# Expert gates of a two-block transformer kernel: one-hot rows made per token with scalar operands

## The chip, the cores and the metric

The kernel runs on one core of a Trainium2 chip. The metric is the device time in microseconds. Three runs of the kernel before gave 3348.83 us (median), between 3345.13 and 3349.56. All rows below come from one profiled execution, whose span is 3351.7 us.

## The reference, cut to what matters

256 tokens of 1024 channels go through a first block (attention and feed-forward layers) and a second block of two layers, each a mixer and then an expert layer (`peer_ffn`). The change touches the expert layer alone:

```python
def peer_ffn(h, w_q, sub_keys, u_tab, v_tab):
    q = (h @ w_q).reshape(B, S, PEER_HEADS, 2, PEER_DQ // 2)
    scores = jnp.einsum('bshpd,hpkd->bshpk', q, sub_keys)
    s1, i1 = lax.top_k(scores[..., 0, :], PEER_TOPK)
    s2, i2 = lax.top_k(scores[..., 1, :], PEER_TOPK)
    ...
    ids = jnp.take_along_axis(cand_id, top_pos, axis=-1)
    gate = jax.nn.softmax(top_s, axis=-1)
    ...
        u = u_tab[idx]
        act = jax.nn.gelu(jnp.einsum('thkd,td->thk', u, hx))
        return jnp.einsum('thk,thkd->td', g * act, v_tab[idx])
```

There are 128 x 128 experts, and a token picks 8 heads x 16 of them. An expert's number has two halves, i1 and i2, each below 128.

## The kernel before, in words

The kernel does not gather experts. For each of 128 tiles of 128 experts it computes the activations of all tokens (`u_tile`, L1661), keeps them in `M` (128 experts of a tile on partitions, 128 tiles, 256 tokens), multiplies them by a dense gate (zero for experts that a token did not pick), and multiplies the result by the second table (`accumulate`, L1358). A tile of u costs 24 products on PE, 8 input channels by 3 passes, since every float32 weight is split into two parts, `hi` and `lo`. `hi` is made by ACT (L262), `lo` by POOL or DVE (L263): in the stretch with gates the pattern `lo_pat` is "PVPVP", three of five on POOL and two on DVE. The weights come over SP's queue in 512 KB pieces; there are three buffers each for `raw`, `hi` and `lo`.

The dense gates are made four tokens at a time (`gates(g)`, 64 groups in a layer). The 128 picks of a token lie on partitions. `CT` holds the two halves of the expert number, `W3` the weight as three bfloat16 parts. Comparing a half with 0 to 127 (`iota`) gives, for each pick, a one-hot row of 128; `oh[:, 0]` has the rows of the second half, `first` those of the first half, and `oh[:, 1:4]` is `first` times the three weight parts. PE multiplies the one-hot matrix of the second half (stationary) with the three weighted ones (moving) into a quarter of a PSUM bank for each token: 12 products for a group. DVE then multiplies the u tiles that are already in `M` by these gates (L1656), and ACT writes the gates into the rest of `M` (L1658), where later u tiles are multiplied in (L1666, L1669, L1670).

Before the change the tile `oh` is laid out [partition, kind, one-hot column, token]: the token is innermost, so a token's row has its elements four apart (8 bytes). Three wide DVE instructions make a group: two compares of 512 elements (L1645) and one multiplication of 1536 (L1646).

A program that schedules by its own costs sets the order in which the instructions of an engine stand; every engine then works through its own in that order. The budgets in the loop (0.85 groups of gates for a u tile) fix the mix of gates and tiles: 27 tiles pass while the picks are found, then about 75 tiles go with the 64 groups, then 26 come alone.

Of the kernel before, what the change touches and what calls it, by code (L numbers as in the profile page):

```python
# [12 lines left out]
BF16 = mybir.dt.bfloat16  # L13
U32 = mybir.dt.uint32
AF = mybir.ActivationFunctionType
ALU = mybir.AluOpType
# [156 lines left out]
class Kernel:  # L173
# [33 lines left out]
    def input_tiles(self):  # L207
        # beside the tokens two columns, for the products with vectors
        self.XHc, self.XLc = (self.cp.tile([128, KT, T + 2], F32R, name=n, tag=n) for n in ("XH", "XL"))
        self.XH, self.XL = self.XHc[:, :, :T], self.XLc[:, :, :T]  # L210
# [29 lines left out]
    def ps(self, tag="mm", n=None):  # L240
        """One of the eight banks: four in turn for each of two uses, or a certain one."""
        if n is None:
            n = self.bank[tag] % 4
            self.bank[tag] += 1
        return self.pp.tile([128, 512], F32, name="ps_" + tag, tag=f"{tag}{n}", bufs=1)

    def lo_engine(self):
        if self.calm:
            # the first weights after a norm: not in the way of its VectorE work
            self.calm -= 1  # L250
            return self.nc.gpsimd
        e = self.lo_pat[self.lo_n % len(self.lo_pat)]
        self.lo_n += 1
        return self.nc.vector if e == "V" else self.nc.gpsimd
# [24 lines left out]
    @contextmanager  # L279
    def stream(self, raw, hi):  # L280
        """More room for the weights on their way while this lasts."""
        with self.tc.tile_pool(name="xraw", bufs=raw) as r, self.tc.tile_pool(name="xhi", bufs=hi) as h:
            self.seq = {"raw": [self.rawp] * 3 + [r] * raw, "hi": [self.hip] * 3 + [h] * hi}
            self.seq_n = {"raw": 0, "hi": 0}
            yield
        self.seq = {"raw": [self.rawp], "hi": [self.hip]}
# [20 lines left out]
    def linear(self, out, wsrc, kt, xin, chunk=8):  # L307
        mm = self.nc.tensor.matmul
        k0 = 0
        # which operand is the last to be there  # L310
        passes = ((0, 0), (1, 0), (0, 1)) if self.fresh else ((0, 0), (0, 1), (1, 0))
        while k0 < kt:
            n = min(chunk, kt - k0)
            w = self.first or self.wsplit(wsrc[:, k0:k0 + n, :], (n, 128))
            self.first = None
            order = [(i, k) for i in range(3) for k in range(n)]
            if self.fresh == "channels":
                # the inputs come, or go, one after the other
                order.sort(key=lambda o: o[1])
            elif self.fresh == "banks":  # L320
                order.sort(key=lambda o: (o[0] == 2, o[1] > 5))
            for at, (i, k) in enumerate(order):
                a, b = passes[i]
                mm(out, w[a][:, k], xin[b][:, k0 + k], start=k0 == 0 and at == 0,  # L324
                   stop=k0 + n == kt and at == 3 * n - 1)
            k0 += n
# [3 lines left out]
    def emit(main, side=(), rate=1.0):  # L330
        """Runs a generator, with the steps of others spread among its own."""
# [14 lines left out]
    def fill(self, n, after):  # L346
        """Some of the work that can be done at any time, but not before a tile is there."""
# [11 lines left out]
    def start(self, weights):  # L359
        """The input, and with it the first weights, in parts."""  # L360
# [23 lines left out]
    def sqrt_soon(self, pool, x):  # L384
        """Loads the square root's table once x is there, ahead of its use."""
# [16 lines left out]
    def layer_norm(self, pool, l, n, mid=(), then=None):  # L402
        """then: "raw" or "mod" if the products after it start before the norm is known (begin)."""
# [98 lines left out]
    def softmax(self, pool, parts, scale, guard, gate=None):  # L502
        """parts: (scores, bias, n) of rows side by side; all their probabilities in one tile."""
# [26 lines left out]
    def causal_pt(self, pool, score, bias, scale, gate=None):  # L530
        """Transposed probabilities: early queries, late queries on early keys, late on late."""
# [22 lines left out]
    def mem_keys(self, l):  # L554
        # one head's rows in each copy, zeros in the other's
# [11 lines left out]
    def natural(self, wsrc, x, store):  # L567
        """256 columns with the tokens on partitions."""
        nc = self.nc
        p = self.ps("ax")  # L570
        for c in range(2):
            hi, lo = self.wsplit(wsrc[:, 4 * c:4 * c + 4], (4, T))
            for k in range(4):
                kk = 4 * c + k
                for a in range(2):
# [3 lines left out]
                    # both halves of the bank form one group: its first product clears them  # L579
# [38 lines left out]
    # The attention of a mixer and its output projection: the sums of the projection stay in four banks, and each  # L618
    # 128 channels are added to them when their heads are done.
    def mix_start(self, l, mix):  # L620
        self.l, self.mix = l, mix
        self.ob = self.ps("ax", 3)
        # in the place of the mixer's input, which is not needed any more
# [7 lines left out]
    def mixed(self):  # L631
        """Half a bank for the outputs of two heads."""
# [4 lines left out]
    def project_out(self, i):  # L637
# [7 lines left out]
        for b in range(4):  # L645
            for w, x in ((hi, xh), (hi, xl), (lo, xh)):
                for k in (0, 1):
                    # the two halves of a bank form one group: its first product clears both
# [32 lines left out]
    def mla(self, l, mid=()):  # L681
        nc, tc, A = self.nc, self.tc, self.A
        with self.stream(2, 2), tc.tile_pool(name="mla", bufs=1) as pool:
# [9 lines left out]
            # per head: 64 rows without position, 32 rotated ones  # L693
            qt = pool.tile([128, 12, T], F32, name="qt")
            kt = pool.tile([128, 12, T], F32, name="kt")
            # what comes before the heads' parts, in their place
# [24 lines left out]
            # keys and values from the latent  # L721
# [21 lines left out]
            for c in range(3):  # L743
                hi, lo = self.wsplit(A["uq"][c], (4, 2, 128))
                # four heads: two tiles without position, their rotated rows, and those swapped
# [42 lines left out]
    def nsa_kv(self, pool, tp):  # L788
# [6 lines left out]
        # one group's rows in each copy, zeros in the other's  # L795
# [70 lines left out]
    def nsa(self, l):  # L866
        nc, tc, A = self.nc, self.tc, self.A
        kk, vv, kc, vc = self.nsakv
        with self.stream(2, 2), tc.tile_pool(name="nsa", bufs=1) as pool:
# [22 lines left out]
            # compressed branch  # L892
# [93 lines left out]
    # The products of a normalised input x r ac + sh start with x ac, before r is known: the products of the  # L986
    # first tiles are multiplied by r (a number per token) and get that of sh, a column beside the tokens, added.
# [30 lines left out]
    def begin(self, pool, srcs, hm=None, norm=True):  # L1018
        """The first products with a normalised input, before its norm is known; then that input in full."""
# [45 lines left out]
    def add_later(self, n=KT):  # L1065
        """What the input lacks yet of the normalised one, which only the residual needs."""
# [13 lines left out]
    def product(self, wsrc, pool, tmp=None):  # L1080
        """A tile of products with the normalised input, and a bias to be added to it."""
# [19 lines left out]
    def rms_sum(self, pool, gains=None):  # L1101
        """The sum of squares for a norm; the last one (with gains) at once for the whole of it."""
        nc, X = self.nc, self.X
        # a norm before this one may have left its shift to be added
# [30 lines left out]
    def hgrn(self, l):  # L1135
        nc, tc, A = self.nc, self.tc, self.A
        with self.stream(2, 1), tc.tile_pool(name="hg", bufs=1) as pool:
# [64 lines left out]
            def project(pr):  # L1202
# [7 lines left out]
                # Q[:, 0]: backward, Q[:, 1]: forward; K[:, 0]: forward, K[:, 1]: backward  # L1210
# [10 lines left out]
            def attend(pr):  # L1221
# [12 lines left out]
                for li, h in enumerate(LEVELS):  # L1234
# [11 lines left out]
                    # products of the decays over blocks of h, then the next level's operands  # L1246
# [75 lines left out]
    def prepare(self):  # L1322
        """What the second block needs from its parameters alone."""
        nc = self.nc
        # HGRN2's lower bounds: softmax over the one layer, then its exclusive sum
# [8 lines left out]
        # the convolution's taps  # L1334
# [5 lines left out]
        # softplus(-lam) = max(-lam, 0) + log1p(exp(-|lam|)), the logarithm by its atanh series  # L1340
# [17 lines left out]
    def accumulate(self, l, i, n, operands, nxt=None):  # L1358
        """Products of n tiles of input channels with all 1024 outputs, which fill four banks, and the residual."""
# [5 lines left out]
        def products(t, k, ops):  # L1365
            hi, lo, xh, xl = ops
            o = acc[k // 2][:, (k % 2) * T:(k % 2 + 1) * T]
            # the two halves of a bank form one group: its first product clears both
# [8 lines left out]
        # the last two tiles finish one bank after the other  # L1377
# [13 lines left out]
    def lru(self, l):  # L1391
        nc, tc, A = self.nc, self.tc, self.A
        with self.stream(3, 3), tc.tile_pool(name="lru", bufs=1) as pool:
# [10 lines left out]
            # zeros that are ready late, as biases, keep the functions of one activation table together  # L1404
# [5 lines left out]
            def conv(i):  # L1410
                for s in range(2):
                    k = 2 * i + s
                    p = self.raws.popleft()
                    # the input without its bias b, and -b where its padding is; b comes with that of the convolution
# [52 lines left out]
            # R holds u/2, u = 8 r softplus(-lam); a = exp(-u), sqrt(-expm1(-2u)) = (1 + a) sqrt(tanh(u/2))  # L1467
# [42 lines left out]
    def peer(self, l):  # L1510
        nc, tc, A = self.nc, self.tc, self.A
        with ExitStack() as st:
# [16 lines left out]
            # queries, scores, the sixteen best of each half  # L1529
# [54 lines left out]
            def decode(a):  # L1584
                # positions to expert halves, and the softmax of the sixteen scores
# [25 lines left out]
            # per token and pair its two halves of the expert's number, and its weight as the sum of three bfloat16  # L1611
            CT = gpool.tile([128, 2, T], BF16, name="CT")
            W3 = gpool.tile([128, 3, T], BF16, name="W3")
            iota4 = gpool.tile([128, 128, 4], BF16, name="iota4")
            nc.vector.tensor_copy(iota4, self.iota[:, :, None].to_broadcast([128, 128, 4]))
# [20 lines left out]
            done = [0, 0]   # u tiles in M, tokens whose gates are in M  # L1636

            def gates(g):
                t0 = 4 * g
                ts = slice(t0, t0 + 4)  # L1640
                # tokens innermost: two bytes an element, all at the fast rate
                oh = gpool.tile([128, 4, 128, 4], BF16, name="oh", tag="oh", bufs=2)
                first = gpool.tile([128, 128, 4], BF16, name="first", tag="first", bufs=1)
                for dst, n in ((first, 0), (oh[:, 0], 1)):
                    nc.vector.tensor_tensor(dst, iota4, CT[:, n, None, ts].to_broadcast([128, 128, 4]), op=ALU.is_equal)  # L1645
                nc.vector.tensor_tensor(oh[:, 1:], first[:, None].to_broadcast([128, 3, 128, 4]),  # L1646
                                        W3[:, :, None, ts].to_broadcast([128, 3, 128, 4]), op=ALU.mult)
                p = self.ps()
                for t in range(4):
                    for n in range(3):  # L1650
                        nc.tensor.matmul(p[:, t * 128:t * 128 + 128], oh[:, 0, :, t], oh[:, 1 + n, :, t],  # L1651
# [184 lines left out]
```

## Time and profile before

| | |
|---|---|
| median of three runs | 3348.83 us |
| lowest, highest | 3345.13, 3349.56 us |
| span of the profiled execution | 3351.7 us |
| PE, PE weight loads | 94%, 92% of the span |
| DVE, ACT, POOL | 77%, 48%, 44% of the span |
| gate products of the first and the second layer | 1511.3 to 1814.5 us, 2596.4 to 2899.5 us |
| gate products in all, DVE instructions that make their operands | 1536, 384 |

In the profile a "busy" DVE also counts time in which an instruction has begun and cannot go on, and durations of instructions that stand back to back overlap a little, so what an instruction costs its engine is read from the distance between starts. PE's durations are longer than its pace for the same reason. Columns of the views are explained with each group of rows below.

### The profile page before, as it was taken

The numbers are of one execution on the slowest core, as the hardware profiler recorded it, in microseconds if no ns is written. First come the engines' busy times: TensorE is split into PE (matmuls) and PEld (weight loads), VectorE is DVE, ScalarE is ACT, GpSimd is POOL, SyncE is SP. The second block draws the span as 40 slices with busy tenths as digits, with TensorE's granted clock in tenths as the row PEclk, the third lists the DMA queues.
The fourth block names the chain that finished last, engine by engine and source line by source line (L and its number), as shares of the span: only waits on it lengthen the run. The fifth ranks groups of instructions, "written<-read, shape, count | busy, mean of one in ns | idle before, by whom it ended". The sixth has DMA issues, their size and how long they took to land.

```text
span 3351.7 us, 63598 instructions
## 1 busy us (share of the span) xinstructions
PE 3159.2 (94%) x25308; PEld 3083.7 (92%) x25308; DVE 2579.4 (77%) x4131; ACT 1620.5 (48%) x2853; POOL 1487.0 (44%) x671
## 2 busy tenths in 40 slices
PE   9999999999899798969999999998696999999998
PEld 9998999998799798959999999997696999999998
DVE  6866967855686886997898666669999889866666
ACT  5456545545554566424434444445442443444444
POOL 5643545653254354743334433335464333433333
PEclk9999999999999899979999999998897999999999
DMA  7853785872286343433344555564243443455554
GB/s 273 287 162 101 258 263 171 301 242 88 89 280 217 94 133 108 145 108 126 128 132 145 183 183 182 184 194 134 87 146 106 133 132 127 146 186 180 187 180 148
DMA packets 155817, 558.78 MB, mean 167 GB/s; under 512 B 17408, under 2 KB 19200, under 8 KB 155264
## 3 DMA queue, kind: packets, MB, share of 16 engines
q1 hardware_dynamic: 155232, 554.19, 50.5%
q8 instruction: 199, 3.26, 0.4%
q14 instruction: 98, 0.80, 0.1%
q10 hardware_dynamic: 288, 0.52, 0.0%
HBM read 553.60 MB, written 1.05 MB: 165 GB/s over the span
## 4 chain that ended last, share of the span: by engine, by line
PE 77%; DVE 17%; ACT 3%; issue 2%; DMA 0%; POOL 0%; SPq 0%; DVEq 0%; ACTq 0%; POOLq 0%
PE ps_mm L324 41%; PE ps_ax L1370 8%; PE ps_ax L1369 8%; PE ps_ax L1371 8%; PE ps_mm L1651 5%; DVE M L1605 2%; DVE M L1607 1%; PE ps_mm L649 1%; DVE lo L263 1%; PE ps_ax L324 1%; DVE M L1574 1%; ACT hi L262 1%; DVE X L1051 1%; DVE RS L1113 1%; DVE M L1609 1%
## 5 line engine op out<-in xcount | busy, mean ns | idle before, releaser
L263 POOL TENSOR_TENSOR lo<-raw,hi 128x1024 fp32r<-128x1024 f32 (+2 forms) x539 | 1335.9, 2483 | 1673.2 <-ACT hi L262 1554.4
L262 ACT ACTIVATE hi<-raw 128x1024 fp32r<-128x1024 f32 (+1 forms) x948 | 986.3, 1047 | 939.5 <-PE ps_mm L324 389.4
L263 DVE TENSOR_TENSOR lo<-raw,hi 128x1024 fp32r<-128x1024 f32 (+2 forms) x420 | 567.6, 1353 | 226.5 <-ACT hi L262 213.5
L324 PE MATMUL ps_mm<-XH,hi 128*128 128x256 f32 (+1 forms) x4056 | 621.1, 292 | 42.2 <-ACT hi L262 22.8
L324 PE MATMUL ps_mm<-XL,hi 128*128 128x256 f32 (+1 forms) x4056 | 594.5, 288 | 9.7 <-DVE XL L1060 5.6
L324 PEld LDWEIGHTS ps_mm<-XH,hi 128*128 128x128 f32 x4056 | 546.5, 195 | 51.2 <-ACT hi L262 23.9
L324 PE MATMUL ps_mm<-XH,lo 128*128 128x256 f32 (+1 forms) x4056 | 586.2, 285 | 3.2 <-DVE lo L263 2.6
L1369 PE MATMUL ps_ax<-ah,hi 128*128 128x256 f32 x2048 | 579.6, 283 | 0.0
L1370 PE MATMUL ps_ax<-al,hi 128*128 128x256 f32 x2048 | 579.6, 283 | 0.0
L1371 PE MATMUL ps_ax<-ah,lo 128*128 128x256 f32 x2048 | 579.6, 283 | 0.0
L324 PEld LDWEIGHTS ps_mm<-XL,hi 128*128 128x128 f32 x4056 | 540.6, 194 | 13.0 <-DVE XL L1060 6.5
L324 PEld LDWEIGHTS ps_mm<-XH,lo 128*128 128x128 f32 x4056 | 534.7, 192 | 4.4 <-DVE lo L263 3.4
L263 DVE TENSOR_TENSOR al<-M,ah 128x256 fp32r<-128x256 f32 x256 | 306.7, 1199 | 167.8 <-ACT ah L262 167.8
L1370 PEld LDWEIGHTS ps_ax<-al,hi 128*128 128x128 f32 x2048 | 393.2, 192 | 0.0
L1371 PEld LDWEIGHTS ps_ax<-ah,lo 128*128 128x128 f32 x2048 | 393.2, 192 | 0.0
L1369 PEld LDWEIGHTS ps_ax<-ah,hi 128*128 128x128 f32 x2048 | 393.2, 192 | 0.0
L1670 DVE TENSOR_TENSOR M<-M,ga 128x256 f32<-128x256 f32 (+34 forms) x198 | 299.2, 1511 | 105.1 <-ACT ga L1669 104.5
L1651 PE MATMUL ps_mm<-oh 128*128 128x128 bf16 x1536 | 203.1, 297 | 0.0
L1658 ACT ACTIVATE M<-ps_mm 128x396 f32<-128x396 f32 (+42 forms) x128 | 48.5, 379 | 292.0 <-DVE M L1656 292.0
L967 DVE SCALAR_TENSOR_TENSOR raw<-raw,one,cb 128x1024 f32<-128x1024 f32 x96 | 183.8, 1914 | 2.9
L1651 PEld LDWEIGHTS <-oh 128*128 128x128 bf16 x1536 | 163.7, 118 | 7.8
L1646 DVE TENSOR_TENSOR oh<-first,W 128x1536 bf16<-128x1536 bf16 x128 | 121.3, 948 | 0.0
(447 smaller groups left out, 4029.0 us busy)
## 6 DMA issues: line engine op xcount, KB each, us to landing
raw<-in_pu_dram SPq DMA_DIRECT2D x256, 512.0 KB, 3.4
raw<-in_pv_dram SPq DMA_DIRECT2D x256, 512.0 KB, 3.7
raw<-in_gu_dram SPq DMA_DIRECT2D x175, 512.0 KB, 4.6
raw<-in_ada_dram SPq DMA_DIRECT2D x96, 512.0 KB, 4.5
raw<-in_down_dram SPq DMA_DIRECT2D x64, 512.0 KB, 4.3
raw<-in_hgin_dram SPq DMA_DIRECT2D x32, 512.0 KB, 3.5
raw<-in_wq_dram SPq DMA_DIRECT2D x32, 512.0 KB, 3.4
raw<-in_down_dram SPq DMA_DIRECT2D x32, 384.0 KB, 3.9
```

The costliest lines, as they stand in the source:

```text
L262: self.nc.scalar.activation(hi, src, AF.Copy)
L263: (eng or self.lo_engine()).tensor_tensor(lo, src, hi, op=ALU.subtract)
L324: mm(out, w[a][:, k], xin[b][:, k0 + k], start=k0 == 0 and at == 0, stop=k0 + n == kt and at == 3 * n - 1)
L967: nc.vector.scalar_tensor_tensor(w, w, tick, cb, op0=ALU.mult, op1=ALU.mult, accum_out=self.MOD[:, l, j:j + 1])
L1369: m(o, hi[:, k], xh, start=t == 0 and k % 2 == 0, stop=False, skip_group_check=True)
L1370: m(o, hi[:, k], xl, start=False, stop=False, skip_group_check=True)
L1371: m(o, lo[:, k], xh, start=False, stop=t == n - 1 and k % 2 == 1, skip_group_check=True)
L1605: nc.vector.tensor_tensor(e[:, h], hb[:, s, h][:, :, None].to_broadcast([128, 16, 16]), io[:, None, :].to_broadcast([128, 16, 16]), op=ALU ...
L1646: nc.vector.tensor_tensor(oh[:, 1:], first[:, None].to_broadcast([128, 3, 128, 4]), W3[:, :, None, ts].to_broadcast([128, 3, 128, 4]), op= ...
L1651: nc.tensor.matmul(p[:, t * 128:t * 128 + 128], oh[:, 0, :, t], oh[:, 1 + n, :, t], start=n == 0, stop=n == 2)
L1658: nc.scalar.activation(M[:, n:, ts], pv[:, n:], AF.Copy)
L1670: nc.vector.tensor_tensor(M[:, i, :n], M[:, i, :n], ga[:, :n], op=ALU.mult)
```

## The change

`oh` becomes [partition, token, kind, one-hot column], so each token's one-hot rows lie in one piece. They are made token by token: one compare for the second half, with the number as a scalar operand (one value per partition), and three instructions that compare the first half with a number and multiply by a weight part, with two scalar operands each. That is 16 instructions of 128 elements for a group in the place of three of 512, 512 and 1536. The tile `first` and the wide copy of `iota` go; a narrow bfloat16 copy stands in their place. PE's instructions are the same in number and size; their operands lie in one piece. Comments are left out of the new file as well.

```diff
-            iota4 = gpool.tile([128, 128, 4], BF16, name="iota4")
-            nc.vector.tensor_copy(iota4, self.iota[:, :, None].to_broadcast([128, 128, 4]))
+            iob = gpool.tile([128, 128], BF16, name="iob")
+            nc.vector.tensor_copy(iob, self.iota)
...
-                oh = gpool.tile([128, 4, 128, 4], BF16, name="oh", tag="oh", bufs=2)
-                first = gpool.tile([128, 128, 4], BF16, name="first", tag="first", bufs=1)
-                for dst, n in ((first, 0), (oh[:, 0], 1)):
-                    nc.vector.tensor_tensor(dst, iota4, CT[:, n, None, ts].to_broadcast([128, 128, 4]), op=ALU.is_equal)
-                nc.vector.tensor_tensor(oh[:, 1:], first[:, None].to_broadcast([128, 3, 128, 4]),
-                                        W3[:, :, None, ts].to_broadcast([128, 3, 128, 4]), op=ALU.mult)
+                oh = gpool.tile([128, 4, 4, 128], BF16, name="oh", tag="oh", bufs=2)
                 p = self.ps()
                 for t in range(4):
+                    at = t0 + t
+                    nc.vector.tensor_scalar(oh[:, t, 0], iob, CT[:, 1, at:at + 1], None, op0=ALU.is_equal)
+                    for n in range(3):
+                        nc.vector.tensor_scalar(oh[:, t, 1 + n], iob, CT[:, 0, at:at + 1], W3[:, n, at:at + 1],
+                                                op0=ALU.is_equal, op1=ALU.mult)
                     for n in range(3):
-                        nc.tensor.matmul(p[:, t * 128:t * 128 + 128], oh[:, 0, :, t], oh[:, 1 + n, :, t],
+                        nc.tensor.matmul(p[:, t * 128:t * 128 + 128], oh[:, t, 0], oh[:, t, 1 + n],
                                          start=n == 0, stop=n == 2)
```

What this does to DVE's order, in the middle of the stretch with gates, is seen between two instructions that multiply `M` by gates (L1656; L1670 multiplies it by a new u tile). The kernel before has there, with the semaphores that each instruction waits for:

```order
L1656 TENSOR_TENSOR M<-M,ps_mm 128x65x4 [waits PE_49]
L1645 TENSOR_TENSOR oh<-iota_15990,CT 128x512
L1646 TENSOR_TENSOR oh<-first,W_15989 128x1536 [waits DVE_49]
L1645 TENSOR_TENSOR first<-iota_15990,CT 128x512 [waits DVE_49]
L1670 TENSOR_TENSOR M<-M,ga 128x128 [waits Activation_49]
L1656 TENSOR_TENSOR M<-M,ps_mm 128x66x4 [waits PE_49]
```

At the same place the changed kernel has, with 16 short instructions for a group:

```order
L1656 TENSOR_TENSOR M<-M,ps_mm 128x65x4 [waits PE_49]
L1646 TENSOR_SCALAR oh<-iob,CT 128x128
L1648 TENSOR_SCALAR oh<-iob,CT,W_15989 128x128 x3
L1646 TENSOR_SCALAR oh<-iob,CT 128x128
L1648 TENSOR_SCALAR oh<-iob,CT,W_15989 128x128 x3
L1646 TENSOR_SCALAR oh<-iob,CT 128x128
L1648 TENSOR_SCALAR oh<-iob,CT,W_15989 128x128 x3
L263 TENSOR_TENSOR lo<-raw,hi 128x1024 [waits DMAHW5_49,Pool_49]
L1670 TENSOR_TENSOR M<-M,ga 128x128 [waits Activation_49]
L1656 TENSOR_TENSOR M<-M,ps_mm 128x66x4 [waits PE_49]
```

The short ones stand between the same two L1656 (twelve of them at this place), and behind them a weight's `lo` (L263), which in the kernel before comes only after the second L1656.

On PE, the kernel before has the 12 products of a group in one run between the runs of a u tile. In the second half of the stretch the changed kernel has single gate products among those of the u tile:

```order
L324 MATMUL ps_mm<-XL,hi 128x256
L1651 LDWEIGHTS oh
L1651 MATMUL ps_mm<-oh 128x128
L324 MATMUL ps_mm<-XH,lo 128x256 x3
L1651 LDWEIGHTS oh
L1651 MATMUL ps_mm<-oh 128x128
L324 MATMUL ps_mm<-XH,lo 128x256
```

There, products of a u tile stand behind gate products that need a single token's rows.

## Rows read from the trace of the kernel before

**Rows 1.** Windows: busy us of each engine, then granted clock, DMA share, GB/s.
```profile
1560.00:1800.00 240.00, 240.00 (x2016) 236.88 (x2015) 212.47 (x284) 97.72 (x227) 84.59 (x35) 1.00 0.40 130
1900.00:2000.00 100.00, 100.00 (x836) 100.00 (x835) 65.98 (x56) 47.67 (x70) 32.70 (x15) 1.00 0.58 182
```

**Rows 2.** Chain that ended last, from 1697 us: start, length, engine and line.
```profile
1698.90 1.43 PE ps_mm L1651 x12
1700.33 2.86 PE ps_mm L324 x24
```

**Rows 3.** Groups of 1560 to 1800: busy us, mean ns | idle before, releaser.
```profile
L1670 DVE TENSOR_TENSOR M<-M,ga 128x44 f32<-128x44 f32 (+49 forms) x59 | 87.4, 1482 | 24.5 <-ACT ga L1669 24.2
L263 POOL TENSOR_TENSOR lo<-raw,hi 128x1024 fp32r<-128x1024 f32 x35 | 84.6, 2417 | 151.5 <-ACT hi L262 132.9 <-ACT M L1666 18.6
...
L262 ACT ACTIVATE hi<-raw 128x1024 fp32r<-128x1024 f32 x59 | 62.5, 1060 | 28.5 <-PE ps_mm L324 23.9 <-issue 4.4
...
L1646 DVE TENSOR_TENSOR oh<-first,W 128x1536 bf16<-128x1536 bf16 x50 | 47.4, 949 | 0.0
L263 DVE TENSOR_TENSOR lo<-raw,hi 128x1024 fp32r<-128x1024 f32 x24 | 29.3, 1221 | 1.3 <-ACT hi L262 1.3
L1656 DVE TENSOR_TENSOR M<-M,ps_mm 128x160 f32<-128x160 f32 (+50 forms) x51 | 22.2, 435 | 0.0
L1645 DVE TENSOR_TENSOR first<-iota,CT 128x512 bf16<-128x512 bf16 x50 | 21.3, 425 | 1.7
L1645 DVE TENSOR_TENSOR oh<-iota,CT 128x512 bf16<-128x512 bf16 x50 | 20.8, 415 | 0.0
```

**Rows 4.** Timeline, one tile and group: start, length, engine, line [idle before, releaser].
```profile
1701.59 0.45 DVE L1656 TENSOR_TENSOR M<-M,ps_mm 128x300 f32<-128x300 f32 x1
...
1701.97 0.41 DVE L1645 TENSOR_TENSOR oh<-iota,CT 128x512 bf16<-128x512 bf16 x1
...
1702.31 0.95 DVE L1646 TENSOR_TENSOR oh<-first,W 128x1536 bf16<-128x1536 bf16 x1
1702.33 1.06 ACT L262 ACTIVATE hi<-raw 128x1024 fp32r<-128x1024 f32 x1
...
1703.46 2.49 POOL L263 TENSOR_TENSOR lo<-raw,hi 128x1024 fp32r<-128x1024 f32 x1 [1.97 <-ACT hi L262]
1703.75 2.40 DVE L1670 TENSOR_TENSOR M<-M,ga 128x160 f32<-128x160 f32 x1
...
1709.24 0.33 DVE L1670 TENSOR_TENSOR M<-M,ga 128x164 f32<-128x164 f32 x1
```

**Rows 5.** DVE instructions by line: duration ns min/median/max, first and last start.
```profile
L1305 DVE TENSOR_SCALAR O<-O,ssq x16: 281/288/292, 1271.5 to 1286.2; 128x128 f32<-128x128 f32 x16
L1452 DVE TENSOR_SCALAR R<-R,spw x16: 340/824/2489, 2302.9 to 2333.6; 128x256 f32<-128x256 f32 x16
L1656 DVE TENSOR_TENSOR M<-M,ps_mm x128: 265/416/572, 1513.0 to 2901.3; 128x116 f32<-128x116 f32 x2, 128x120 f32<-128x120 f32 x2, 128x124 f32<-128x124 f32 x2, 128x128 f32<-128x128 f32 x2
L1219 DVE TENSOR_TENSOR Q<-q,f x8: 678/680/687, 1141.0 to 1249.5; 128x512 f32<-128x512 f32 x8
```

**Rows 6.** Timeline of DVE: short instructions with scalars, back to back.
```profile
1285.61 0.88 DVE L1305 TENSOR_SCALAR O<-O,ssq 128x128 f32<-128x128 f32 x4
...
1139.59 0.73 DVE L1216 TENSOR_SCALAR f<-f,lb 128x256 f32<-128x256 f32 x2
1140.24 0.48 DVE L1096 SCALAR_TENSOR_TENSOR pt<-pt,pb,RS 128x256 f32<-128x256 f32 x1
...
1410.68 0.22 DVE L1595 TENSOR_SCALAR M<-M 128x128 uint32<-128x128 uint32 x1
1410.81 0.22 DVE L1596 TENSOR_SCALAR M<-M 128x128 uint32<-128x128 uint32 x1
```

**Rows 7.** Windows where PE's pace is held up by other engines; columns as in rows 1.
```profile
1210.00:1220.00 10.00, 10.00 (x57) 8.55 (x57) 10.00 (x14) 6.07 (x12) 6.14 (x4) 1.00 0.32 102
1430.00:1440.00 10.00, 0.47 (x1) 0.18 (x1) 10.00 (x21) 0.00 (x0) 1.83 (x1) 0.60 0.33 105
```

## The prediction

> **What bounds the kernel now.** I read the windows first, to see which engine is full in the stretch with gates: in the 240 us from 1560 to 1800 PE is busy all the time at full granted clock, with 2016 products, 0.119 us each; in the stretch that has u tiles alone it is 836 in 100 us, 0.120 each [rows 1]. The chain of work that ended last says the same: a tile's 24 products take 2.86 us and a group's 12 take 1.43, both 0.119 a product [rows 2]. So a gate product that streams 128 bfloat16 columns with gaps costs PE as much as one that streams 256 columns without. 59 tiles and 50 groups make 59 x 2.86 + 50 x 1.43 = 240 us. PE sets the pace here, and the change would shorten only the 1.43.
>
> How far the other engines are behind PE is read from the groups of the same 240 us [rows 3]. ACT, which starts each weight's split, waits 23.9 us for PE to give buffers back, so without PE the rest would need about 216. That can be counted in a second way. A DVE instruction with its operands in SBUF and a POOL instruction do not run side by side: POOL's L263 runs from 1703.46 to 1705.95, and DVE's L1670 takes 2.40 us from 1703.75, to 1706.15, where one of the same kind and nearly the same size takes 0.33 [rows 4]; a short multiplication by a scalar takes 340 ns at least and 2489 at most [rows 5]. L1656, which reads PSUM, never takes over 572 [rows 5] and is left out. The two engines then need, one after the other:
> - L1670 at its own price, 59 x 0.33 = 19.5 us;
> - DVE's L263, 29.3 us;
> - the three instructions of a group, by the distance between starts: 0.34 for the first compare [rows 4], 0.95 and 0.42 for the others [rows 3], 1.71 us, 50 times: 85.5 us;
> - POOL's L263, 84.6 us.
>
> The sum is 218.9 us, close to the 216. DVE and POOL together thus stand at 91% of PE's time, and 21 us in 50 groups, 0.42 us for a group, is all that they can take on before they set the pace.
>
> **The change, part by part.** *PE:* 12 products of a group read packed rows. No row here shows a packed bfloat16 product of this size. From above its price is the present 0.119 (the gaps cost nothing); from below half of it, 0.06, as 128 columns are half of 256. A group would save up to 0.7 us. As long as DVE and POOL are later, this is worth nothing.
>
> *DVE, removed:* 1.71 us for a group. *Added:* 16 instructions, four with one scalar operand and twelve with two. The trace has neighbours in float32. One scalar, 128 columns: four of L1305 in a row take 0.88 us, the last one 0.29, so starts are (0.88 - 0.29) / 3 = 0.197 us apart [rows 6, 5]. Two scalars, 256 columns: two of L1216 take 1140.24 - 1139.59 = 0.65 us until the next instruction starts, 0.325 each [rows 6]. With constants in the instruction, 128 columns: 0.13 (L1595 to L1596) [rows 6]. A scalar read from SBUF thus costs some 0.06 us. 128 columns more cost 340 - 281 = 59 ns in the one-scalar form [rows 5]. Bfloat16 halves the price of a column in the two-tensor form: 949 - 415 = 534 ns for 1024 columns more, against 1221 - 680 = 541 for 512 in float32 [rows 3, 5]; I take the same for the new form, 0.03 us for 128 columns. One scalar: 0.197 - 0.03 = 0.167 us. Two: 0.325 - 0.059 - 0.03 = 0.236. A group: 4 x 0.167 + 12 x 0.236 = 3.50 us, 1.79 more than before. Bounds: if the second scalar costs nothing, 16 x 0.167 = 2.67; if columns keep the float32 price, 3.98.
>
> *The sum:* 218.9 + 50 x 1.79 = 308.4 us in the place of 240, so 68.4 / 50 = 1.37 us for a group; 128 groups make 175 us. Set against the profiled execution, 3351.7 + 175 = 3527. The median of the runs is 3 us below that span, so 3524. The cheap bound gives 218.9 + 50 x 0.96 = 266.9, 0.54 us a group, 69 us: 3418. The dear one adds 0.48 us a group, 61 us; and if L1656 finds no POOL instruction to run beside, 22.2 / 50 = 0.44 more, 57 us: 3642 with both.
>
> *Moves:* behind the short instructions in DVE's order stand L263 (two of five weights' `lo`), L1670 and L1656; L1656 releases ACT's L1658 and with it the next `hi`, and PE waits for these at the end. PE's single gate products in the second half put u-tile products behind one token's rows; that adds no work. The smaller `iob` copy and the freed `first` are worth under 1 us.
>
> **Rivals.** *Faster: short instructions cost only their columns.* The place is the same pair DVE and POOL. It stays below PE's 240 if a group's operands cost at most 1.71 + 0.42 = 2.13 us, 0.133 an instruction; that is the price of the form with constants, 0.13. If scalars were read beside the columns, an instruction would cost 0.13 - 0.03 = 0.10, a group 1.6, the pair 213 us; with PE at 0.06 a gate product, 240 - 600 x 0.06 = 204, the pair would bound: -27 us in 50 groups, -68 in all, 3281. L1305 and L1216 speak against it. [...]
>
> *Not held by POOL.* If the new instructions, with one tensor each, ran beside POOL, DVE alone would count: 19.5 + 29.3 + 175 + 22.2 = 246 us, 15 us over in all, 3364; with its waits for ACT of 24.5 us [rows 3], 270.5, 78 us, 3424. The 2489 ns of L1452, one tensor and one scalar, speak against it.
>
> *Far slower.* If the new form takes a column at the float32 two-tensor price, 541 / 512 = 1.06 ns, a group costs 16 x 0.105 = 1.7 us more: 3740. Or the granted clock falls as PE waits: it was 0.60 where PE had one product in 10 us, but 1.00 with 57, which is less than the 65 or so that the forecast leaves [rows 7]. If 60% of the stretch ran at half the clock, PE would need 240 x 1.6 = 384 us, 369 us more, about 3720.
>
> *No change.* The slack is larger than both counts say: 3349.
>
> **How the numbers follow.** The pair as bound at the scalar prices, 3419 to 3642 with 3524 in the middle: 0.68. A nearly free second scalar, 3400 to 3419: 0.08. Not held by POOL, 3364 to 3424: 0.07. Far slower: 0.09. Faster: 0.05. No change: 0.03. The range of 8 in 10 takes the first two and the upper half of the third: 3402 to 3640. A measurement here tells about 0.2% from no change; slower by more than that is 0.68 + 0.08 + 0.07 + 0.09 = 0.92, faster 0.05, the same 0.03.
>
> **What would show it.** In the windows of the stretch with gates, PE's count falls from 2016 in 240 us to about 1570, and DVE is busy all the time. L1648 starts about 0.24 us after its predecessor and L1646 0.17, with cases of over 2 us where POOL holds them. ACT no longer waits for PE; PE waits for POOL's or DVE's `lo` and for `oh`. L1651 pairs may be shorter than 0.119 without any gain. The prediction is wrong if L1648 comes every 0.13 us or less, if it runs beside POOL, or if the stretch lasts under 310 us a layer, where it took 303.

## The result, and the profile after

The changed kernel takes 3515.38 us (median of 4 runs, 3514.76 to 3526.34) against 3348.14; the ratio is 1.051, 95% interval 1.0495 to 1.0525. The forecast was 3524, range 3402 to 3640. The profiled execution spans 3513.0 us, 161.3 more than that of before.

All of the loss lies in the two stretches with gates. These are PE's gate products there, the first layer's and the second's (duration in ns, then first and last start):

```profile
L1651 PE MATMUL ps_mm<-oh x768: 216/219/330, 1508.0 to 1896.7; 128*128 128x128 bf16 x192
L1651 PE MATMUL ps_mm<-oh x768: 216/219/330, 2669.7 to 3064.0; 128*128 128x128 bf16 x192
```

The stretches last 388.7 and 394.3 us, where they took 303.2 and 303.1: 176.7 us more. The parts ahead of, between and behind them are shorter by 3.3, 8.9 and 3.2 us, since the first products start earlier and the last ones stand nearer to the end of the u tiles. 176.7 - 15.4 = 161.3.

The window that answers to the first of [rows 1], with the same columns:

```profile
1560.00:1800.00 240.00, 204.20 (x1580) 184.40 (x1578) 230.69 (x720) 77.89 (x177) 69.17 (x29) 0.91 0.31 102
```

PE, full before, now has 1580 products in the place of 2016 and idles; DVE goes from 212 to 231 us. The groups of the same 240 us, to be read against [rows 3], show who waits for whom:

```profile
L1648 DVE TENSOR_SCALAR oh<-iob,CT,W 128x128 bf16<-128x128 bf16 x462 | 148.5, 367 | 0.0
L263 POOL TENSOR_TENSOR lo<-raw,hi 128x1024 fp32r<-128x1024 f32 x29 | 69.9, 2413 | 174.7 <-ACT hi L262 104.1 <-PE ps_mm L1651 39.6 <-DVE oh L1648 21.8
L1651 PE MATMUL ps_mm<-oh 128*128 128x128 bf16 x459 | 67.8, 227 | 35.8 <-DVE oh L1648 34.6
...
L1646 DVE TENSOR_SCALAR oh<-iob,CT 128x128 bf16<-128x128 bf16 x155 | 58.6, 378 | 0.0
...
L1651 PEld LDWEIGHTS <-oh 128*128 128x128 bf16 x459 | 34.4, 99 | 40.9 <-DVE oh L1646 19.1 <-issue 4.8 <-DVE oh L1648 4.0
L1670 DVE TENSOR_TENSOR M<-M,ga 128x44 f32<-128x44 f32 (+39 forms) x47 | 22.1, 470 | 6.4 <-ACT ga L1669 6.1 <-ACT M L1658 0.2
L263 DVE TENSOR_TENSOR lo<-raw,hi 128x1024 fp32r<-128x1024 f32 x17 | 20.6, 1210 | 0.0
L1656 DVE TENSOR_TENSOR M<-M,ps_mm 128x160 f32<-128x160 f32 (+38 forms) x39 | 15.8, 405 | 2.9 <-PE ps_mm L1651 2.9
```

PE's gate products, which waited for nothing before, wait 34.6 us for L1648, and their weight loads 19.1 for L1646. The short DVE instructions wait for no semaphore (0.0) but last 367 and 378 ns on average, above their medians of 303 and 243 ns in the two stretches. Where that comes from is seen on the timeline of POOL and DVE:

```profile
1607.34 0.24 DVE L1646 TENSOR_SCALAR oh<-iob,CT 128x128 bf16<-128x128 bf16 x1
1607.50 0.75 DVE L1648 TENSOR_SCALAR oh<-iob,CT,W 128x128 bf16<-128x128 bf16 x3
1608.07 2.44 POOL L263 TENSOR_TENSOR lo<-raw,hi 128x1024 fp32r<-128x1024 f32 x1 [4.93 <-ACT hi L262]
1608.17 2.40 DVE L1646 TENSOR_SCALAR oh<-iob,CT 128x128 bf16<-128x128 bf16 x1
1610.49 0.75 DVE L1648 TENSOR_SCALAR oh<-iob,CT,W 128x128 bf16<-128x128 bf16 x3
```

The L1646 of 1608.17 begins just after POOL's L263 and lasts 2.40 us, until it ends. Before, it was L1670 that POOL held (mean 1482 ns); now L1670 has 470 and the short instructions have the wait. Behind it three L1648 take 0.75 us, and a token's four take 0.83 (from 1603.60 to 1604.43 below). DVE holds POOL too: in the kernel before, POOL's L263 of 50.79 us, begun 0.05 us after an L263 of DVE that takes 1.23, lasts 3.43 us, where its median is 2.40.

With that price the pair of DVE and POOL, counted as the prediction counted it, all but fills the window: 47 x 0.33 for L1670, 20.6 for DVE's L263, 39 groups x 4 x 0.83 and 69.9 for POOL's L263 make 235.5 of the 240 us. DVE's own parts without POOL's, with 15.8 for L1656, would make 181.

### The profile page after: what moved, and what is told of

It reads as the page before. It is cut to its first block, busy times and chain, and to the rows that moved or that the text cites. A ratio compares the mean times of both kernels' runs of the same rounds, so it can differ in the third digit from the quotient of the medians.

```text
span 3513.0 us, 65227 instructions
## 1 busy us (share of the span) xinstructions
PE 3212.6 (91%) x25308; PEld 3072.9 (87%) x25308; DVE 2794.7 (80%) x5795; ACT 1622.5 (46%) x2853; POOL 1490.4 (42%) x671
## 5 line engine op out<-in xcount | busy, mean ns | idle before, releaser
L263 POOL TENSOR_TENSOR lo<-raw,hi 128x1024 fp32r<-128x1024 f32 (+2 forms) x539 | 1339.1, 2490 | 1833.1 <-ACT hi L262 1559.0
L263 DVE TENSOR_TENSOR lo<-raw,hi 128x1024 fp32r<-128x1024 f32 (+2 forms) x420 | 574.5, 1369 | 218.0 <-ACT hi L262 206.4
L324 PE MATMUL ps_mm<-XH,hi 128*128 128x256 f32 (+1 forms) x4056 | 659.5, 300 | 36.2 <-ACT hi L262 16.2
L324 PE MATMUL ps_mm<-XL,hi 128*128 128x256 f32 (+1 forms) x4056 | 642.5, 298 | 9.6 <-DVE XL L1060 4.4
L324 PEld LDWEIGHTS ps_mm<-XH,hi 128*128 128x128 f32 x4056 | 571.1, 199 | 76.3 <-issue 24.5
L324 PE MATMUL ps_mm<-XH,lo 128*128 128x256 f32 (+1 forms) x4056 | 616.0, 292 | 5.3 <-DVE lo L263 4.4
L324 PEld LDWEIGHTS ps_mm<-XL,hi 128*128 128x128 f32 x4056 | 574.7, 201 | 32.0 <-issue 19.4
L324 PEld LDWEIGHTS ps_mm<-XH,lo 128*128 128x128 f32 x4056 | 557.5, 198 | 18.3 <-issue 10.1
L1648 DVE TENSOR_SCALAR oh<-iob,CT,W 128x128 bf16<-128x128 bf16 x1536 | 504.0, 374 | 0.0
L263 DVE TENSOR_TENSOR al<-M,ah 128x256 fp32r<-128x256 f32 x256 | 306.7, 1199 | 167.2 <-ACT ah L262 167.2
L1651 PE MATMUL ps_mm<-oh 128*128 128x128 bf16 x1536 | 247.6, 229 | 110.4 <-DVE oh L1648 106.7
L1651 PEld LDWEIGHTS <-oh 128*128 128x128 bf16 x1536 | 120.9, 99 | 119.5 <-DVE oh L1646 48.4
L1646 DVE TENSOR_SCALAR oh<-iob,CT 128x128 bf16<-128x128 bf16 x512 | 191.3, 374 | 0.0
```

The source lines that it names most:

```text
L263: (eng or self.lo_engine()).tensor_tensor(lo, src, hi, op=ALU.subtract)
L1646: nc.vector.tensor_scalar(oh[:, t, 0], iob, CT[:, 1, at:at + 1], None, op0=ALU.is_equal)
L1648: nc.vector.tensor_scalar(oh[:, t, 1 + n], iob, CT[:, 0, at:at + 1], W3[:, n, at:at + 1], op0=ALU.is_equal, op1=ALU.mult)
L1651: nc.tensor.matmul(p[:, t * 128:t * 128 + 128], oh[:, t, 0], oh[:, t, 1 + n], start=n == 0, stop=n == 2)
```

## Experiments

Theory A is the prediction's: DVE and POOL, which hold each other up, set the pace of the stretch, because a scalar operand read from SBUF adds about 0.06 us to each short instruction. The rivals say that PE alone matters, that the gaps were free, that it is the number of instructions that costs, or that DVE is full by itself and POOL runs beside it.

### PE's packed rows alone, and DVE's new instructions alone

`packed_reads` is the kernel before with packed reads of PE out of the same tile:

```diff
+                flat = oh.rearrange("p k c t -> p (k c t)")
...
-                        nc.tensor.matmul(p[:, t * 128:t * 128 + 128], oh[:, 0, :, t], oh[:, 1 + n, :, t],
+                        nc.tensor.matmul(p[:, t * 128:t * 128 + 128], flat[:, t * 128:t * 128 + 128],
+                                         flat[:, (4 + 3 * t + n) * 128:(5 + 3 * t + n) * 128],
```

> The kernel before, in which PE reads its gate operands as packed rows of 128 out of the same tile, at the same number of products; DVE's three wide instructions stay. The rows that PE then multiplies are not the tokens' (the gates have no meaning), the work is otherwise the whole. Theory A (DVE and POOL exclude each other and stand at 219 of PE's 240 us; packed rows halve a gate product): PE falls to 240 - 50 x 0.77 = 201 us, the pair bounds at 219, 21 / 50 x 128 = 54 us less: 3294. Rival B (PE alone sets the pace, nothing else is near): all of 0.77 x 128 = 99 us less: 3250. Rival C (the gaps cost PE nothing): 3348.

`gapped_reads` is the changed kernel with PE's operands read four apart:

```diff
+                    gap = oh[:, t].rearrange("p k c -> p (k c)").rearrange("p (c k) -> p c k", k=4)
...
-                        nc.tensor.matmul(p[:, t * 128:t * 128 + 128], oh[:, t, 0], oh[:, t, 1 + n],
+                        nc.tensor.matmul(p[:, t * 128:t * 128 + 128], gap[:, :, 0], gap[:, :, 1 + n],
```

> The changed kernel, in which PE reads its gate operands four elements apart as before the change; DVE's 16 short instructions stay. The gates have no meaning, the work is otherwise the whole. Theory A: the pair of DVE and POOL bounds at about 300 us in the place of 240, PE at 240 is under it, so nothing is lost: 3515, within 15. Rival B (PE and DVE work one after the other, so that packed rows gave back 99 us of what DVE lost): 3515 + 99 = 3614.

Measured: 3282.27 us for `packed_reads` (ratio 0.9798, 0.9781 to 0.9814), 3514.07 for `gapped_reads` (1.0487, 1.0469 to 1.0504). So the packed rows by themselves are worth 69 us, not nothing and not 99, and in the changed kernel they are worth nothing: without them it takes the same time. Two windows, `packed_reads` first, then `gapped_reads`:

```profile
1560.00:1800.00 240.00, 232.63 (x2230) 227.82 (x2229) 232.72 (x298) 104.78 (x250) 99.46 (x40) 1.00 0.42 146
```

```profile
1560.00:1800.00 240.00, 209.23 (x1593) 196.70 (x1592) 229.51 (x714) 78.29 (x180) 70.36 (x29) 0.93 0.29 100
```

With packed rows PE is no longer full (232.6), and DVE is busy for 232.7 us of the 240 in the place of 212. These two alone do not tell which of them bounds; the pair's parts in the window of `packed_reads` do (L1672 is the L1670 of before):

```profile
L1672 DVE TENSOR_TENSOR M<-M,ga 128x256 f32<-128x256 f32 (+31 forms) x66 | 103.5, 1572 | 4.5 <-ACT ga L1671 2.6
L263 POOL TENSOR_TENSOR lo<-raw,hi 128x1024 fp32r<-128x1024 f32 x40 | 99.5, 2487 | 142.7 <-ACT hi L262 103.6 <-ACT M L1668 22.6 <-PE ps_mm L324 8.5
...
L1646 DVE TENSOR_TENSOR oh<-first,W 128x1536 bf16<-128x1536 bf16 x51 | 48.3, 947 | 0.0
...
L263 DVE TENSOR_TENSOR lo<-raw,hi 128x1024 fp32r<-128x1024 f32 x26 | 31.6, 1216 | 0.5 <-ACT hi L262 0.5
```

66 x 0.33 + 31.6 + 51 x 1.71 + 99.5 = 240 us, all of the window: the pair has become the bound. 69 us in 128 groups are 27 in 50, which puts it at 213 us for what took PE 240, where the prediction counted 219 and 216.

### Which operand's gaps cost

`packed_moving` packs only the weighted rows (moving), `packed_stationary` only the compared ones; in the second argument `oh[:, 0, :, t]` stays, or in the third `oh[:, 1 + n, :, t]`.

> The kernel before, in which PE reads only the moving operand of the gate products (the weighted rows) as packed rows; the stationary one keeps its gaps. The gates have no meaning. If the moving operand's gaps are what doubles a gate product: products of 219 ns and 3282 us, as with both packed. If the stationary operand's gaps are: products of 297 ns and 3350 us.

> The kernel before, in which PE reads only the stationary operand of the gate products (the compared rows) as packed rows; the moving one keeps its gaps. The gates have no meaning. If the moving operand's gaps are what doubles a gate product: products of 297 ns and 3350 us, weight loads of 97 ns in the place of 117. If the stationary operand's gaps are: products of 219 ns and 3282 us.

One run each: 3285.8 us and 3349.77, beside 3349.43 for the kernel before. Weight loads and products of `packed_moving`, then of `packed_stationary` (ns, minimum, median, maximum):

```profile
L1652 PEld LDWEIGHTS <-oh x1536: 110/113/137, 1510.8 to 2831.8; 128*128 128x128 bf16 x192
L1652 PE MATMUL ps_mm<-oh x1536: 218/219/250, 1510.8 to 2831.8; 128*128 128x128 bf16 x192
```

```profile
L1652 PEld LDWEIGHTS <-oh x1536: 96/115/118, 1513.0 to 2895.7; 128*128 128x128 bf16 x192
L1652 PE MATMUL ps_mm<-oh x1536: 274/294/296, 1513.0 to 2895.8; 128*128 128x128 bf16 x192
```

The gain is the moving operand's: 219 ns against 294. The stationary operand's gaps cost a load some 20 ns at most (117 before, 97 or 98 where nothing has gaps of four), and the kernel nothing that one run shows. (The expected 97 ns for the packed load was the minimum, not the median.)

### What makes the short instructions dear

`constants` puts numbers in the place of the scalar operands, `one_scalar` only in the place of the weight:

```diff
-                    nc.vector.tensor_scalar(oh[:, t, 0], iob, CT[:, 1, at:at + 1], None, op0=ALU.is_equal)
+                    nc.vector.tensor_scalar(oh[:, t, 0], iob, 5.0, None, op0=ALU.is_equal)
...
-                        nc.vector.tensor_scalar(oh[:, t, 1 + n], iob, CT[:, 0, at:at + 1], W3[:, n, at:at + 1],
+                        nc.vector.tensor_scalar(oh[:, t, 1 + n], iob, 7.0, 0.125,
```

```diff
-                        nc.vector.tensor_scalar(oh[:, t, 1 + n], iob, CT[:, 0, at:at + 1], W3[:, n, at:at + 1],
+                        nc.vector.tensor_scalar(oh[:, t, 1 + n], iob, CT[:, 0, at:at + 1], 0.125,
```

> The changed kernel with constants in the place of all scalar operands of the 16 short instructions (the gates have no meaning); number, size and place of the instructions stay. Theory A (a scalar read from SBUF costs 0.06 us): 0.10 us an instruction, 1.6 a group, the pair falls to 219 - 5 = 214 us and PE to 201: 26 / 50 x 128 = 67 us under the kernel before, 3281. Rival D (it is the number of instructions that costs, whatever their operands): 3515.

> The changed kernel with the weight part as a constant in the place of the second scalar operand; the compare keeps its scalar (the gates have no meaning). Theory A (each scalar read from SBUF has its own price, 0.165 us an instruction with one, 0.225 with two): 16 x 0.165 = 2.64 us a group, 0.71 under the changed kernel, 128 x 0.71 = 91 us less: 3424. Rival F (the first scalar costs all, the second comes with it): 3515. Rival G (only the second costs): about 3280, as with constants.

Measured: 3277.72 us (0.9783, 0.9767 to 0.98) and 3390.07 (1.0119, 1.0103 to 1.0136). With the same 16 instructions of the same size the kernel is 2.2% faster or 5.1% slower than before, by where their operands come from. (The order of DVE's instructions, which the scheduling program sets, is not quite the same in these runs; the prices below do not depend on it.) Timelines of DVE, of the changed kernel, of `one_scalar` and of `constants`; the price is the distance from one start to the next:

```profile
1603.60 0.24 DVE L1646 TENSOR_SCALAR oh<-iob,CT 128x128 bf16<-128x128 bf16 x1
1603.76 0.75 DVE L1648 TENSOR_SCALAR oh<-iob,CT,W 128x128 bf16<-128x128 bf16 x3
1604.43 0.24 DVE L1646 TENSOR_SCALAR oh<-iob,CT 128x128 bf16<-128x128 bf16 x1
```

```profile
1702.55 0.24 DVE L1646 TENSOR_SCALAR oh<-iob,CT 128x128 bf16<-128x128 bf16 x1
1702.71 0.57 DVE L1648 TENSOR_SCALAR oh<-iob,CT 128x128 bf16<-128x128 bf16 x3
1703.20 0.24 DVE L1646 TENSOR_SCALAR oh<-iob,CT 128x128 bf16<-128x128 bf16 x1
```

```profile
1701.80 0.38 DVE L1648 TENSOR_SCALAR oh<-iob 128x128 bf16<-128x128 bf16 x3
1702.11 0.18 DVE L1646 TENSOR_SCALAR oh<-iob 128x128 bf16<-128x128 bf16 x1
1702.21 0.38 DVE L1648 TENSOR_SCALAR oh<-iob 128x128 bf16<-128x128 bf16 x3
```

With two scalars 0.67 / 3 = 0.223 us, with one 0.49 / 3 = 0.163 (0.16 for L1646 too), with none 0.31 / 3 = 0.103. Each scalar has its own price of 0.06 us; rivals F and G fall. `one_scalar` came out 34 us below what was expected, because that was reckoned from the changed kernel, which also loses time to waits: DVE is busy all 240 us of the window in `one_scalar`, and 231 in the changed kernel. The window of `one_scalar`:

```profile
1560.00:1800.00 240.00, 215.31 (x1852) 201.69 (x1851) 240.00 (x847) 85.46 (x207) 80.97 (x33) 0.94 0.35 117
```

From the pair's sum it is 218.9 + 50 x (16 x 0.163 - 1.71) = 263.8 us, 23.8 / 50 x 128 = 61 in all over the kernel before; less the 15 by which the parts outside the stretches shrank in the changed kernel that is 46, measured 41. That the two are so close is partly luck: in the profiled executions the stretches grew by 43 us and not 61, and the other parts shrank by 11 and not 15.

### Whether POOL holds DVE

`lo_on_dve` is the changed kernel with `self.lo_pat = "V"` for "PVPVP" in the stretch; `before_lo_on_dve` is the same edit in the kernel before.

> The changed kernel, in which all lo parts of the stretch with gates are made by DVE and none by POOL; the result is the same. Theory A (POOL's 2.4 us hold DVE for as long, so the same part is cheaper on DVE at 1.2): 19.5 + 59 x 1.2 + 50 x 3.35 + 22.2 = 280 us in the place of 300, 40 / 50 x 128 = 102 us over the kernel before: 3450. Rival E (DVE alone is the bound and POOL runs beside it): 35 x 1.2 = 42 us more in 50 groups, 108 in all: 3623.

> The kernel before, in which all lo parts of the stretch with gates are made by DVE; the result is the same. Theory A: PE bounds at 240 us with gapped rows whatever the others do: 3350, no change. Rival (the pair already costs something here): up to 20 us less.

Measured: 3414.54 us (1.0196, 1.0179 to 1.0213) and 3341.2 (0.9974, 0.9964 to 0.9983). Giving a full DVE the lo parts that POOL had made, some 90 in the two stretches, makes the changed kernel 101 us faster, since each takes 1.2 us and ends a hold of 2.4. Rival E, at 3623, falls. DVE stays the bound, busy for 232 of 240 us:

```profile
1560.00:1800.00 240.00, 220.67 (x1751) 190.58 (x1749) 232.06 (x844) 92.05 (x196) 0.00 (x0) 1.00 0.32 112
```

The gain is larger than reckoned. The first stretch of `lo_on_dve` ends at 1847.0 us and the second at 2963.2, 343 us each in the place of 303: 80 us more than in the kernel before, where 102 were reckoned. The parts outside are 19 us shorter, as they were by 15 in the changed kernel. The sum's prices were a little high, as DVE's timeline shows by the distance between starts:

```profile
1701.12 0.32 DVE L1670 TENSOR_TENSOR M<-M,ga 128x152 f32<-128x152 f32 x1 [0.21 <-ACT ga L1669]
1701.35 0.53 DVE L1648 TENSOR_SCALAR oh<-iob,CT,W 128x128 bf16<-128x128 bf16 x2
...
1703.46 1.21 DVE L263 TENSOR_TENSOR lo<-raw,hi 128x1024 fp32r<-128x1024 f32 x1
1704.60 0.45 DVE L1656 TENSOR_TENSOR M<-M,ps_mm 128x292 f32<-128x292 f32 x1
1704.97 1.21 DVE L263 TENSOR_TENSOR lo<-raw,hi 128x1024 fp32r<-128x1024 f32 x1
```

L1670 costs 0.23 us where the sum has 0.33, a lo 1.14 for 1.2, L1656 0.37 for 22.2 / 50 = 0.44. First and last gate product of `lo_on_dve`, then of `before_lo_on_dve`, whose first and second stretch stand one under the other:

```profile
L1651 PE MATMUL ps_mm<-oh x768: 216/229/233, 1504.0 to 1847.0; 128*128 128x128 bf16 x192
L1651 PE MATMUL ps_mm<-oh x768: 216/229/233, 2619.9 to 2963.2; 128*128 128x128 bf16 x192
```

```profile
L1651 PE MATMUL ps_mm<-oh x768: 283/297/304, 1507.4 to 1810.5; 128*128 128x128 bf16 x192
L1651 PE MATMUL ps_mm<-oh x768: 283/297/304, 2583.5 to 2886.6; 128*128 128x128 bf16 x192
```

The kernel before gains 8 us from the edit, which theory A did not have; but its stretches last 303.1 us as ever, and the gain lies ahead of them (in the profiled executions, which lie 13 us apart, 3.9 us before the first and 8.9 between the two), nearly where the changed kernel gained 3.3 and 8.9. What in the order of the work there gives this was not tried.

### A version that beats both

If a step of two is still cheap for PE, tokens in pairs keep DVE's wide instructions and give PE what it needs. `token_pairs` lays `oh` out [partition, pair, kind, column, 2]; `token_pairs_lo_on_dve` has `lo_pat` "V" beside it:

```diff
+                oh = gpool.tile([128, 2, 4, 128, 2], BF16, name="oh", tag="oh", bufs=2)
+                first = gpool.tile([128, 2, 128, 2], BF16, name="first", tag="first", bufs=1)
+                for j in range(2):
+                    tj = slice(t0 + 2 * j, t0 + 2 * j + 2)
+                    for dst, n in ((first[:, j], 0), (oh[:, j, 0], 1)):
+                        nc.vector.tensor_tensor(dst, iota2, CT[:, n, None, tj].to_broadcast([128, 128, 2]),
+                                                op=ALU.is_equal)
+                    nc.vector.tensor_tensor(oh[:, j, 1:], first[:, j, None].to_broadcast([128, 3, 128, 2]),
+                                            W3[:, :, None, tj].to_broadcast([128, 3, 128, 2]), op=ALU.mult)
...
+                        nc.tensor.matmul(p[:, t * 128:t * 128 + 128], oh[:, t // 2, 0, :, t % 2], oh[:, t // 2, 1 + n, :, t % 2],
```

> The kernel before with the tokens innermost in pairs and no longer in fours, so a token's row has its elements two apart; six DVE instructions of 256 and 768 elements in the place of three; the result is the same. DVE: 4 x 0.21 + 2 x 0.55 = 1.94 us a group in the place of 1.71. Theory A with a step of two costing PE nothing: the pair, which the run with packed reads puts at 240 - 69 x 50 / 128 = 213 us, rises by 12 to 225, 15 / 50 x 128 = 38 us less than before: 3311. Rival H (any gap costs PE the double): 3350, no change.

> The pairs of tokens, and all lo parts of the stretch with gates on DVE; the result is the same. Theory A: DVE alone counts, 19.5 + 59 x 1.2 + 50 x 1.94 + 22.2 = 209 us by the price that held before, and 14 less if it overrates as in the run with lo on DVE (3450 expected, 3415 measured); PE at 201 to 209: 31 to 39 us in 50 groups, 79 to 100 in all: 3250 to 3270. Rival E (DVE is the bound by itself, POOL runs beside it): 42 us more in 50 groups than token_pairs, 3418.

Measured: 3303.61 us (0.9866, 0.985 to 0.9883) and 3252.14 (0.9711, 0.9695 to 0.9728). Gate products and window of `token_pairs`, then the window of `token_pairs_lo_on_dve` and two pieces of its chain that ended last:

```profile
L1654 PEld LDWEIGHTS <-oh x1536: 96/97/103, 1506.0 to 2845.8; 128*128 128x128 bf16 x192
L1654 PE MATMUL ps_mm<-oh x1536: 217/218/236, 1506.0 to 2845.9; 128*128 128x128 bf16 x192
```

```profile
1560.00:1800.00 240.00, 226.53 (x2113) 217.22 (x2112) 235.36 (x442) 99.79 (x241) 90.84 (x38) 1.00 0.41 136
```

```profile
1560.00:1800.00 240.00, 240.00 (x2301) 237.74 (x2301) 209.56 (x483) 115.74 (x255) 0.00 (x0) 1.00 0.47 156
```

```profile
1696.46 0.70 PE ps_mm L1654 x12
1697.16 2.91 PE ps_mm L324 x24
```

A step of two costs PE nothing (218 ns, as packed); rival H falls. Where PE is full, a group's 12 products now take 0.70 us, 0.058 each, half of the 1.43 of [rows 2]. In `token_pairs` PE is not full (226.5 of 240 us), the pair bounds, and the gain stays below that of `packed_reads`. With POOL out of the way PE is full again, with 2301 products in the place of 2016, 2.9% faster than the kernel before.

## Why the prediction was right

*The bound.* The step that carried it, that DVE and POOL stood at 219 us against PE's 240 [rows 3], held: `packed_reads` puts the pair at 213, and its parts fill that run's window.

*The price of a group.* Foreseen 4 x 0.167 + 12 x 0.236 = 3.50 us out of float32 neighbours [rows 5, 6]; it is 4 x 0.83 = 3.32. The two-scalar form, 0.223, was 0.013 us below its estimate.

*The sum.* 308 us for 50 groups were foreseen, 68 over the kernel before. The two stretches give (388.7 + 394.3) x 50 / 128 = 306, 69 over theirs before. That it is so close is partly luck, for three errors cancel: the pair before stood at 213 and not at 219, 6 less; a group costs 3.32 and not 3.50, 9 less in 50; and DVE stood idle for 9.3 us of the window, 12 more in 50 groups, which the sum did not have (among them the waits of L1670 for ACT and of L1656 for PE). The 15 us that the other parts gave back were not foreseen either.

*PE.* 1570 products in 240 us were foreseen, 1580 came. Its gate products got shorter, from 297 to 219 ns, and that was worth nothing, as forecast: `gapped_reads`. Of the two bounds for a packed product, 0.06 and 0.119 us, the lower was right. PE's moving operand with a step of 8 bytes makes the product slower (294 against 219 ns, and 64 us of the kernel's time between `packed_stationary` and `packed_moving`), with a step of 4 it does not (218 ns in `token_pairs`).

*Two things were wrong.* The granted clock was expected to stay at 1.00, by a row with even fewer products [rows 7]; it was 0.91 in the window, while PE stood idle for 36 of the 240 us; read in steps of 1 us from 1600 to 1661, it is 1.00 in 44 of them, 0.50 in 12 and between the two in 5. No run separates what this cost, since the clock of `gapped_reads` was as low (0.93). It can hardly have been more than the 9.3 us in which DVE stood idle, and in `one_scalar`, at 0.94, DVE was never idle. And the time of the rival "Not held by POOL" with DVE's waits is off by a slip: 78 us over 3349 are 3427, not 3424.

*The rivals.* The break-even of the faster one, 0.133 us an instruction, fits what was measured on both sides of it: `constants`, at 0.103, gave 3278 where it said 3281, `one_scalar`, at 0.163, is slower than before. "Not held by POOL" is refuted by the timeline and by `lo_on_dve`.

## What to carry to other kernels

Before a cheaper operand is bought for the engine that bounds, count how far the next one is behind: here it was 0.42 us for a group, and the new operand cost 1.6. Short DVE instructions are priced by the distance between starts, form by form; two scalars read from SBUF more than doubled the price of one of 128 columns (0.223 us against 0.103). Where DVE and POOL hold each other up, the same split can cost less on DVE (here 1.2 us against a hold of 2.4), even when DVE is the busier one.

## What the runs showed of the hardware that I had not expected

- The step of PE's moving operand: four bfloat16 apart, 294 to 297 ns a product, 0.119 us from one to the next where PE is full; packed, 219 ns; two apart, 218 ns and 0.058 us. The stationary operand may have gaps of four (113 to 117 against 97 or 98 ns a load, and no time of the kernel that one run shows). Other steps and widths were not tried.
- A scalar operand in SBUF costs a short DVE instruction 0.06 us, as reckoned, and a second one as much again: 0.103, 0.163, 0.223.
- Work moved from POOL to a full DVE made the kernel 101 us faster.
